# Fused column pairs in five input groups of a one-core encoder layer, turns by way of DRAM, and an account of engine time for the side work

## The chip, the cores and the metric

The kernel runs on one core of one Trainium2 chip. The metric is the device time of one execution in microseconds; the time before is a median of 1603.3 us over three runs (1602.81 to 1603.57). Engines are named as in the profile: PE (matrix products), PEld (its weight loads), DVE (vector), ACT (scalar), POOL (GpSimd) and SP (the queue that issues most DMAs).

## The reference

One layer on x of 256 rows and 4096 columns, all in float32:

```
xn = rms_norm(x) * norm_g
h  = xn @ w_in                                   # 4096 x 14336
c_val, c_glu, c_gate, q, k, v, a_gate = split(h) # 2048 columns each
conv = swish(layer_norm(depthwise_conv31(c_val * sigmoid(c_glu)) + conv_b)) * silu(c_gate)
q, k = rms_norm per head (16 heads of 128)
attn = mixture over three dilated windows of softmax(q k^T / sqrt(128) + bias) v
y    = x + concat(conv, attn * silu(a_gate)) @ w_out   # 4096 x 4096
```

With 256 positions the three patterns and the relative bias become one table by distance, `bias_rows`, added to the scores of each head.

## The kernel before, in words

**Products.** Both large products are cut into groups of 1024 output columns (two halves e of 512): 14 input groups (`GROUPS`: four `conv`, then `agv` and `qk` in turn four times, two `gate`) and four `out` groups. The contraction runs over 32 tiles of 128 (k), two to a pair j; one DMA on SP brings the 1 MB of weights of a pair (`load_pair`, three buffers `raw`). Each float32 operand is split into a rounded high part and a low rest (ACT casts, DVE subtracts: `split_w`, L204 and L205), and a product is three matmuls, high x high, low x high, high x low, in PSUM. An ordinary k-step is 2 row halves x 2 column halves x 3 = 12 matmuls of 128 x 512 (`products`, L662 to L665); a plain pair is 24. The input groups multiply x * norm_g and bring in 1/rms only where PSUM is emptied (`evacuate`). Split tiles have eight slots (`ws`), so three k-steps of weights are split ahead.

**Fused pairs.** In each out group the pairs in `FUSED` (six of 16) are multiplied as 2 x 2 blocks with seven block products instead of eight, 21 matmuls instead of 24. That needs sums of blocks of the left side (`mix_fuse`, tiles `mx`) and of the weights (`split_fused`, steps one to four, with helper tiles `t13` and `t24`), four more PSUM banks (`more`, on the `side` banks in the first out group) and `add_more`, which puts the block sums together. `OUT_ORDERS` says in which order an out group takes its pairs.

**Side work.** The depthwise convolution (`conv_gen`, 31 steps on DVE for each of 16 channel tiles), the norm over channels (`ln_gen`), the norms of q and k (`qk_norm`), the 16 heads (`head_gen`, products `psc` and `po` on `side` banks), the gates (`gate_post`, `ag_post`) and the splits of the mixed result (`mix_split_gen`) are Python generators in four lanes. `pump` is called once in each k-step of the input groups; it adds a fixed quota of DVE and ACT time (`STEP`, `GATE_STEP`) and lets the generators issue until the cost that they report has used it up. The lane `fg` steps its first three generators, in order; the convolution comes last and takes what is left. All engines work strictly in the order in which these instructions are issued; there is no other scheduler.

**Turns.** A tile of rows by columns is turned to columns by rows with a DVE transpose inside blocks of 32 x 32 and then 16 ACT copies that move the blocks (`turn`, L307 and L315; for the probabilities L499 and L505). This is done for four conv tiles, four gates, four attention gates, q and k of four head groups, and the probabilities of 16 heads.

Of the kernel before, what the change touches and what calls it, by code (L numbers as in the profile page):

```python
# [17 lines left out]
P = 128  # L18
# [15 lines left out]
STEP, GATE_STEP = (950, 1400), (1300, 1600)  # L34
AHEAD = 3
RAW = 3
XN_LOAD = {1 + (5 * c + 1) // 2: c for c in range(8)}
# [13 lines left out]
FUSED = (0, 1, 2, 3, 4, 5)  # L51
OUT_ORDERS = [(8, 9, 10, 0, 6, 1, 11, 2, 7, 3, 12, 4, 13, 5, 14, 15)]
OUT_ORDERS += 3 * [(8, 9, 0, 10, 1, 11, 2, 6, 3, 7, 4, 12, 5, 13, 14, 15)]
# [5 lines left out]
def _relative():  # L59
# [4 lines left out]
    for m in range(NDEL):  # L64
        d = m - (S - 1)
# [12 lines left out]
        c = int(n <= 64) + int(n % 4 == 0 and n <= 256) + int(n % 16 == 0 and n <= 1024)  # L78
        pattern[m] = math.log(c) if c else NEG
# [3 lines left out]
class Lane:  # L83


    def __init__(self, width):
        self.gens = deque()
        self.width = width

# [3 lines left out]
    def step(self, left):  # L93

        spent = 0
        for gen in list(self.gens)[: self.width]:
            if min(left) <= 0:
# [7 lines left out]
            for i in range(2):  # L105
                left[i] -= cost[i]
# [5 lines left out]
def layer_kernel(  # L112
# [17 lines left out]
    def t4(name):  # L130
        return sb.tile([P, 4, 256], F32, tag="c4", bufs=15, name=name)
# [13 lines left out]
    def rsqrt(src, shape, mul, eps, name):  # L145
# [6 lines left out]
        cost = 60 + n  # L152
# [24 lines left out]

    raw_tiles = {}

    def load_pair(j, cuts=(0, 2048), between=None):  # L180

        g, jj = divmod(j, n_pairs)
        if g >= NG:
            return
        if groups[g][0] == "out":
            jj = (OUT_ORDERS[g - n_in][jj] + n_pairs // 2) % n_pairs
# [7 lines left out]
    w_split = {}  # L194

    def ws(name):
        return sb.tile([P, 1024], F32R, tag="ws", bufs=W_SLOTS, name=name)

    def split_w(n):
        j, kk = divmod(n, 2)  # L200
        src = raw_tiles[j][:, kk]
        wh, wl = ws(f"wh{n}"), ws(f"wl{n}")
        if n:
            nc.scalar.copy(wh, src)  # L204
            nc.vector.tensor_sub(wl, src, wh.bitcast(F32))  # L205
        else:
            a, b = slice(0, 512), slice(512, 1024)
            nc.vector.tensor_copy(wh[:, a], src[:, a])
            split_x(0)
            nc.scalar.copy(wh[:, b], src[:, b])  # L210
            for c in (a, b):
                nc.vector.tensor_sub(wl[:, c], src[:, c], wh[:, c].bitcast(F32))
        w_split[n] = (wh, wl)
        if kk == 1:
            del raw_tiles[j]
            load_pair(j + RAW)

    xh, xl = {}, {}
# [30 lines left out]
    def split_x(k):  # L249
# [6 lines left out]
        xh[k], xl[k] = h, l  # L256

    state = {}

    def finish_rstd():  # L260
# [5 lines left out]
        state["rstd"] = [keep[:, s : s + 1] for s in range(2)]  # L266

# [24 lines left out]
    def backwards(ap):  # L292

        *lead, (step, n) = ap.ap
        return bass.AP(
            tensor=ap.tensor, offset=ap.offset + (n - 1) * step, ap=[*lead, [-step, n]]
        )

    def turn(tile_, name, flip=False):


# [4 lines left out]
        for s in range(2):  # L306
            nc.vector.transpose(flat[:, 512 * s : 512 * s + 512], src[:, 512 * s : 512 * s + 512])  # L307
            yield 620
        blocks = flat.rearrange("p (s t b x) -> p s t b x", s=2, t=4, b=4)
        dst = src.rearrange("p (t s a x) -> p s t a x", t=4, s=2, a=4)  # L310
        for b in range(4):
            for a in range(4):
                v = blocks[32 * a : 32 * a + 32, :, :, b, :]
                to = 3 - a if flip else a
                nc.scalar.copy(  # L315
                    dst[32 * b : 32 * b + 32, :, :, to, :], backwards(v) if flip else v
                )
            yield 0, 1240
# [7 lines left out]
    def conv_gen(cb):  # L326
# [4 lines left out]
        for tp in range(0, 4, 2):  # L331
            for t in (tp, tp + 1):
# [5 lines left out]
                yield 335  # L338
            for k in range(TAPS):
# [4 lines left out]
                for t in (tp, tp + 1):  # L344
# [5 lines left out]
                    yield 335  # L350
# [4 lines left out]
    def channel_mean(srcs, name):  # L355

        tot = sb.tile([P, S], F32, tag="rs_big", bufs=6, name=name + "tot")
        for i, make in enumerate(srcs):
            v = make()
            if i:  # L360
                part = sb.tile([P, S], F32, tag="rs_big", bufs=6, name=f"{name}p{i}")
            else:
                part = tot
            nc.vector.reduce_sum(part, v.rearrange("p t s -> p s t"), axis=AX.X)
            yield 1135
            if i:
                nc.vector.tensor_add(tot, tot, part)
                yield 335
# [9 lines left out]
    def ln_gen():  # L378
        pm = yield from channel_mean([lambda cb=cb: cT[cb] for cb in range(4)], "mu")
# [3 lines left out]
        for cb in range(4):  # L383
            nc.vector.tensor_sub(cT[cb], cT[cb], bcast4(mu))
            yield 1135

        def square(cb):
            sq = t4(f"sq{cb}")
            nc.scalar.activation(sq, cT[cb], AF.Square)
            return sq  # L390

        pv = yield from channel_mean([lambda cb=cb: square(cb) for cb in range(4)], "va")
        r = yield from rsqrt(pv[:, :S], [P, S], 1.0, LN_EPS, "rc")
        for cb in range(4):
            nc.vector.tensor_mul(cT[cb], cT[cb], bcast4(r))
            yield 1135
        for cb in range(4):
            for t in range(4):
# [5 lines left out]
                if t % 2 == 1:  # L404
                    yield 900
# [4 lines left out]
    def gate_post(cb, g):  # L410
        yield
        yield from turn(g, f"turn_g{cb}")
        while cb not in conv_done:
            yield
        for t in range(4):
            nc.vector.tensor_mul(cT[cb][:, t, :], cT[cb][:, t, :], g[:, t, :])
            mix_ready[NH + 4 * cb + t] = cT[cb][:, t, :]
            yield 335

    def ag_post(hg, ag):  # L420
        yield
        yield from turn(ag, f"turn_ag{hg}")
# [5 lines left out]
    def qk_norm(hg):  # L428
        st = sb.tile([P, 16], F32, tag="rs_small", bufs=6, name=f"ssqk{hg}")
        both = (qt[hg], kt[hg])  # L430
        for i, src in enumerate(both):
            sq = t4(f"sq{hg}_{i}")
            nc.scalar.activation(sq, src, AF.Square)
            yield 0, 1000
            yield
            for s in range(2):
                o = 8 * i + 4 * s
                v = sq.rearrange("p a b -> p (a b)")[:, 512 * s : 512 * s + 512]
                nc.vector.reduce_sum(
                    st[:, o : o + 4], v.rearrange("p (h d) -> p h d", h=4), axis=AX.X  # L440
                )
                yield 600
        r = yield from rsqrt(st, [P, 16], 1.0 / DH, NORM_EPS, f"rqk{hg}")
        for i, src in enumerate(both):
            for s in range(2):
                v = src.rearrange("p a b -> p (a b)")[:, 512 * s : 512 * s + 512]
                v = v.rearrange("p (h d) -> p h d", h=4)
                a = r[:, 8 * i + 4 * s : 8 * i + 4 * s + 4]
                rb = bass.AP(tensor=a.tensor, offset=a.offset, ap=[a.ap[0], [1, 4], [0, DH]])
                nc.vector.tensor_mul(v, v, rb)  # L450
                yield 600
        yield from turn(qt[hg], f"turn_q{hg}", flip=True)
        yield from turn(kt[hg], f"turn_k{hg}")
        yield
        nc.vector.tensor_scalar_mul(kt[hg], kt[hg], gqk)
        yield 650
        qk_ready[hg] = True

    def head_gen(hg, hh):
        h = 4 * hg + hh  # L460
        hs = slice(DH * hh, DH * hh + DH)
        while hg not in qk_ready:
# [6 lines left out]
                offset=bias_dram.offset + h * NDEL,  # L469
# [4 lines left out]
        for it in range(2):  # L474
            nc.tensor.matmul(  # L475
                psc[:, it, :], qt[hg][:, hh, P * it : P * it + P], kt[hg][:, hh, :],
# [5 lines left out]
        window = bass.AP(tensor=T.tensor, offset=T.offset + P, ap=[T.ap[0], [-P, 2], [1, 256]])  # L482
# [4 lines left out]
        yield 1200  # L487
# [5 lines left out]
        yield 0, 700  # L493
        nc.vector.reciprocal(z, z)
        for it in range(2):
            nc.vector.tensor_scalar_mul(pi[:, it, :], pi[:, it, :], z[:, it : it + 1])
        yield 600
        tmp = t2(f"turn_p{h}")
        nc.vector.transpose(tmp, pr)  # L499
        yield 620  # L500
# [507 lines left out]
```

## Time and profile before

| | |
|---|---|
| median of three runs | 1603.3 us |
| the profiled execution, its time / its span | 1603.12 / 1601.3 us |
| PE, PEld busy | 1590.5, 1312.8 us |
| DVE, ACT, POOL busy | 1195.0, 968.2, 0.2 us |
| DMA | 323.53 MB, mean 202 GB/s |
| granted PE clock, mean | 0.998 |

A row of a group of instructions gives line, engine, operation, output<-inputs, shapes and count; then busy us and the mean ns of one; then idle us just before them and what ended most of it. Rows of windows give a stretch in us and for each engine its busy time and number of instructions. A row of DMA issues gives the size of one and the median us from issue to landing. Matmuls are pipelined: the duration of one overlaps the next, and the pace is read from the starts.

### The profile page before, as it was taken

To read this page: it belongs to the slowest core of one execution; us is meant where nothing else is said; L and a number is where in the kernel's file an instruction comes from. 1 tells how busy PE (TensorE), PEld (TensorE's weight loads), DVE (VectorE), ACT (ScalarE), POOL (GpSimd) and SP (SyncE) were. 2 spreads that over 40 slices of the span, in tenths; PEclk is the share of its full clock that TensorE was granted. 3 is DMA by queue.
4 is the path that set the end of the run, shared out by engine and by line. 5 is a ranking of instruction groups with operands and counts; after the bars stand their busy time and mean duration, and the time that the engine had idled before them with its cause. 6 is when DMAs were issued, how large, how long until landed. Compare 5 with 4: busy or idle time off the path is not lost.

```text
span 1601.3 us, 18984 instructions
## 1 busy us (share of the span) xinstructions
PE 1590.5 (99%) x6986; PEld 1312.8 (82%) x6986; DVE 1195.0 (75%) x1630; ACT 968.2 (60%) x1480; POOL 0.2 (0%) x4
## 2 busy tenths in 40 slices
PE   9999999999999999999999999999999999999999
PEld 7888888888888888888888888888878877888887
DVE  6668888888888887678755556555467889888886
ACT  6763534445453467755779557754789865545453
POOL 0000000000000000000000000000000000000000
PEclk9999999999999999999999999999999999999999
DMA  9755555555555555555555555455545556665653
GB/s 377 289 184 198 196 186 201 192 184 207 188 190 204 184 195 191 186 186 191 179 195 189 192 203 190 173 187 207 194 163 190 184 210 232 232 229 215 248 198 143
DMA packets 52892, 323.53 MB, mean 202 GB/s; under 512 B 5792, under 2 KB 8480, under 8 KB 16192
## 3 DMA queue, kind: packets, MB, share of 16 engines
q1 hardware_dynamic: 52512, 322.05, 56.4%
q8 instruction: 54, 0.88, 0.2%
q10 hardware_dynamic: 288, 0.28, 0.1%
q14 instruction: 38, 0.31, 0.1%
HBM read 318.08 MB, written 4.23 MB: 201 GB/s over the span
## 4 chain that ended last, share of the span: by engine, by line
PE 96%; ACT 1%; DVE 1%; issue 0%; DMA 0%; DVEq 0%; ACTq 0%
PE acc L662 25%; PE acc L663 25%; PE acc L665 25%; PE c L784 5%; PE c L782 5%; PE c L783 5%; PE m L784 1%; PE m L782 1%; PE m L783 1%; PE po L514 1%; PE psc L475 1%; ACT gate L315 0%; ACT pr L505 0%; DMA first_x<-in_x_cols_dram 0%; DVE t24l L736 0%
## 5 line engine op out<-in xcount | busy, mean ns | idle before, releaser
L205 DVE TENSOR_TENSOR wl<-raw,wh 128x1024 fp32r<-128x1024 f32 x447 | 546.9, 1224 | 336.9 <-ACT wh L204 335.9
L204 ACT CAST wh<-raw 128x1024 fp32r<-128x1024 f32 x447 | 469.6, 1052 | 434.9 <-PE acc L663 241.5
L662 PE MATMUL acc<-wh,xh 128*128 128x512 f32 x1792 | 703.8, 393 | 1.3 <-ACT xh L252 1.3
L663 PE MATMUL acc<-wh,xl 128*128 128x512 f32 x1792 | 698.4, 390 | 0.0
L665 PE MATMUL acc<-wl,xh 128*128 128x512 f32 x1792 | 483.7, 389 | 0.0
L662 PEld LDWEIGHTS acc<-wh,xh 128*128 128x128 f32 x1792 | 337.0, 188 | 72.3 <-ACT xh L252 1.6
L663 PEld LDWEIGHTS acc<-wh,xl 128*128 128x128 f32 x1792 | 336.8, 188 | 70.1 <-DVE xl L253 0.2
L665 PEld LDWEIGHTS acc<-wl,xh 128*128 128x128 f32 x1792 | 336.3, 188 | 70.3
L346 DVE SCALAR_TENSOR_TENSOR cT<-conv,wT,cT 128x241 f32<-128x241 f32 (+14 forms) x480 | 201.6, 471 | 0.0
L782 PE MATMUL c<-oh,mh 128*128 128x512 f32 x320 | 125.3, 391 | 0.5 <-ACT oh L716 0.5
L784 PE MATMUL c<-ol,mh 128*128 128x512 f32 x320 | 125.1, 391 | 0.5 <-DVE ol L717 0.5
L783 PE MATMUL c<-oh,ml 128*128 128x512 f32 x320 | 125.0, 391 | 0.0
L716 ACT CAST oh<-raw 128x1024 fp32r<-128x1024 f32 x80 | 83.2, 1051 | 50.8 <-PE c L783 34.4
L717 DVE TENSOR_TENSOR ol<-raw,oh 128x1024 fp32r<-128x1024 f32 x80 | 96.1, 1222 | 21.8 <-ACT oh L716 15.2
L505 ACT COPY pr<-turn_p 32x128 f32<-32x128 f32 x256 | 75.9, 297 | 9.2 <-DVE turn_p L499 5.7
L782 PEld LDWEIGHTS c<-oh,mh 128*128 128x128 f32 x320 | 60.5, 189 | 13.5 <-ACT oh L716 1.0
L784 PEld LDWEIGHTS c<-ol,mh 128*128 128x128 f32 x320 | 60.3, 189 | 13.5 <-DVE ol L717 1.0
L783 PEld LDWEIGHTS c<-oh,ml 128*128 128x128 f32 x320 | 60.5, 189 | 12.8
L732 ACT CAST t24h<-t 128x1024 fp32r<-128x1024 f32 x24 | 25.2, 1051 | 40.3 <-PE c L783 24.1
L736 DVE TENSOR_TENSOR t24l<-t,t24h 128x1024 fp32r<-128x1024 f32 x24 | 29.4, 1226 | 17.3 <-ACT t24h L732 17.3
L732 ACT CAST t13h<-t 128x1024 fp32r<-128x1024 f32 x24 | 25.3, 1053 | 18.2 <-DVE t L748 14.2
L732 ACT CAST bh<-raw 128x1024 fp32r<-128x1024 f32 x24 | 25.3, 1053 | 16.3 <-PE m L783 16.3
(195 smaller groups left out, 1030.8 us busy)
## 6 DMA issues: line engine op xcount, KB each, us to landing
raw<-in_w_dram SPq DMA_DIRECT2D x286, 1024.0 KB, 4.8
x<-in_x_dram SPq DMA_DIRECT2D x8, 512.0 KB, 7.4
xr<-in_x_dram SPq DMA_DIRECT2D x8, 512.0 KB, 6.0
out_dram<-xr SPq DMA_DIRECT2D x15, 256.0 KB, 2.9
xT<-in_x_cols_dram SPq DMA_DIRECT2D x7, 512.0 KB, 6.9
T<-bias_dram SPq DMA_DIRECT2D x16, 192.0 KB, 5.0
raw<-in_w_dram SPq DMA_DIRECT2D x3, 512.0 KB, 6.2
raw<-in_w_dram SPq DMA_DIRECT2D x2, 256.0 KB, 4.4
```

Of the source, the lines that this page charges most:

```text
L204: nc.scalar.copy(wh, src)
L205: nc.vector.tensor_sub(wl, src, wh.bitcast(F32))
L346: nc.vector.scalar_tensor_tensor(c[:, t, lo:hi], a[:, t, lo + sh : hi + sh], wT[:, ch, k : k + 1], c[:, t, lo:hi], op0=ALU.mult, op1=ALU.add,)
L505: nc.scalar.copy(dst[32 * b : 32 * b + 32, :, :, 3 - a, :], backwards(blocks[32 * a : 32 * a + 32, :, :, b, :]),)
L662: nc.tensor.matmul(a, hs, wp, start=k == 0, stop=False)
L663: nc.tensor.matmul(a, ls, wp, start=False, stop=False)
L665: nc.tensor.matmul(a, hs, wp, start=False, stop=k == KT - 1)
L716: nc.scalar.copy(h, src)
L717: nc.vector.tensor_sub(l, src, h.bitcast(F32))
L782: nc.tensor.matmul(acc, a[0], b[0], start=start, stop=False)
L783: nc.tensor.matmul(acc, a[1], b[0], start=False, stop=False)
L784: nc.tensor.matmul(acc, a[0], b[1], start=False, stop=stop)
```

## The change

1. The input groups 2 to 6 (`FUSED_IN`) take the pairs 2, 4, 6, 8 as fused pairs. The first out group fuses two pairs (0 and 1) instead of six, the other three six as before; the order of the first out group is new. One class `Stream` now splits all weights, of plain groups too.
2. Block sums across rows need normalized x. So in group 1 x is loaded again (eight DMAs of 512 KB), scaled by norm_g and by 1/rms in a row (which goes out to DRAM and comes back to all partitions), split again (`split_xn`), and the sums are made (`block_sums`). From group 2 on nothing is scaled when PSUM is emptied. A fused input group uses all eight PSUM banks; `evacuate_sum` adds the last banks to what `add_more` left.
3. The heads start only once the fused input groups are done (`state["side"]`), since these use the `side` banks.
4. Turns of q, k, both gates and the probabilities go through DRAM: DVE transposes the blocks, then POOL issues one write and four reads (`through_dram`); the generator gives way five times (`LANDING`) before the result is used. The conv tiles keep the ACT copies.
5. The quotas are replaced by an account: each matmul credits 0.93 of 227 ns to DVE and to ACT (`credit`), every instruction, the weight splits too, is taken off (`spend`), and at most 700 ns are carried over. The reported costs are raised.
6. The norms of q and k and the scaling of q and of the probabilities move from DVE to ACT; the sums over channels are additions of whole tiles instead of reductions; `t13` and `t24` are written in place into `raw`; helper tiles `c4` are 18 instead of 15, the DMA scratch is smaller; 11 warm-up products instead of 7; the load of x for the output sums stands at slot 7 instead of 9.

```diff
-STEP, GATE_STEP = (950, 1400), (1300, 1600)
+PRODUCT = 227
+FILL, SAVED = (0.93, 0.93), (700, 700)
+LANDING = 5
+C4 = 18
...
-FUSED = (0, 1, 2, 3, 4, 5)
-OUT_ORDERS = [(8, 9, 10, 0, 6, 1, 11, 2, 7, 3, 12, 4, 13, 5, 14, 15)]
+FUSED_IN = range(2, 7)
+FUSED = [(2, 4, 6, 8) if g in FUSED_IN else () for g in range(N_IN)] + [range(2)] + 3 * [range(6)]
+ORDERS = N_IN * [range(16)]
+ORDERS += [(8, 9, 10, 11, 6, 7, 2, 3, 0, 12, 1, 13, 14, 4, 5, 15)]
...
+    def credit(ns):
+        for i in range(2):
+            left[i] += FILL[i] * ns
...
+    def split_xn(k):
+        src = xT[k]
+        nc.vector.scalar_tensor_tensor(
+            src, src, g_cols[:, k : k + 1], state["rstd_row"], op0=ALU.mult, op1=ALU.mult
+        )
+        yield 480
+        h, l = new_split(k, "n")
+        nc.scalar.copy(h, src)
+        yield 0, 400
+        nc.vector.tensor_sub(l, src, h.bitcast(F32))
+        xh[k], xl[k] = h, l
+        yield 415
+        if k % 2 and k // 2 in FUSED[FUSED_IN[0]]:
+            yield from block_sums(k // 2, src_of=xT, parts=(xh, xl), out=xsum, name="xs")
...
+    def through_dram(src, dst, n, name):
+        d = tc.dram_tile([P, 4 * n], F32, name=name + "d")
+        nc.gpsimd.dma_start(d, src)
+        for b in range(4):
+            nc.gpsimd.dma_start(
+                dst[32 * b : 32 * b + 32, :].rearrange("p (a n) -> p a n", a=4),
+                bass.AP(
+                    tensor=d.tensor,
+                    offset=d.offset + b * n,
+                    ap=[[4 * n, 32], [P * n, 4], [1, n]],
+                ),
+            )
+        for _ in range(LANDING):
+            yield
...
-        while hg not in qk_ready:
+        while hg not in qk_ready or not state["side"]:
             yield
...
-        blocks = tmp.rearrange("p (i j b x) -> p j i b x", i=2, j=2, b=4)
-        dst = pr.rearrange("p (j i a x) -> p j i a x", j=2, i=2, a=4)
-        for b in range(4):
-            for a in range(4):
-                nc.scalar.copy(
-                    dst[32 * b : 32 * b + 32, :, :, 3 - a, :],
-                    backwards(blocks[32 * a : 32 * a + 32, :, :, b, :]),
-                )
-            yield 0, 800
+        yield 700
+        yield from through_dram(tmp, pr, 128, f"turn_p{h}")
...
+    def pump(more=0):
+        credit(more)
+        gate_lane.step(left, spend)
+        fg.step(left, spend)
         for _ in range(2):
-            mix_lane.step(left)
+            mix_lane.step(left, spend)
         for _ in range(8):
-            if not conv_lane.step(left):
+            if not conv_lane.step(left, spend):
                 break
+        for i in range(2):
+            left[i] = min(left[i], SAVED[i])
...
             def one():
-                t13 = kept["t13"] = t4(f"t13_{u}").rearrange("p a b -> p (a b)").rearrange(
-                nc.vector.tensor_sub(t13, r[:, 1:4:2, :], r[:, 0:2, :])
+                both("b", r[:, 0:3:2, :], ("b11", "b21"))
+                nc.vector.tensor_add(r[:, 0:2, :], r[:, 0:2, :], r[:, 1:4:2, :])
+                spend(1225)
...
+            if g == FUSED_IN[0] - 1:
+                if k % 4 == 0:
+                    load_xT(k, 4, nc.sync)
+                if k >= 2:
+                    split_gens.append(split_xn(k - 2))
+                split_more()
             pump()
```

More of the change, by code (lines that the diff above doesn't have):

```diff
@@ L104, in step @@
             cost = cost if isinstance(cost, tuple) else (cost, 0)
-            for i in range(2):
-                left[i] -= cost[i]
+            spend(*cost)
             spent += sum(cost)
@@ L192, in load_pair @@
                 between()
[L194 to L218, printed above, removed]
+    xh, xl, xsum = {}, {}, {}
     def new_split(k, nm):
@@ L452, in qk_norm @@
[L452 to L456, printed above, removed]
+            v = src.rearrange("p a b -> p (a b)")
+            for n in range(8):
+                w_ = v[:, DH * n : DH * n + DH]
+                nc.scalar.activation(
+                    w_, w_, AF.Copy, scale=r[:, 8 * i + n : 8 * i + n + 1]
+                )
+                if n % 4 == 3:
+                    yield 0, 1600
@@ L698, in free, with step @@
                 self.held[tag] -= 1
[L700 to L702 removed]
+        def step(self):
+            if not self.todo or sum(self.held.values()) + self.todo[0][0] > W_SLOTS + self.more:
                 return False
@@ L781, in triple, with bank @@
+            def four():
+                both("t24", blocks()[:, 0:2, :], ("t2", "t4"))
+            return [(2, one), (1, two), (2, three), (2, four)]
+        def bank(self, g, name, tag):
+            return ps.tile([P, 512], F32, tag=tag, bufs=4, name=f"{name}_{g}")
         def triple(self, acc, a, b, start, stop):
@@ L948, in layer_kernel @@
     progress["in"] = KT + 2
-    out.run()
+    mix_lane.engines = ()
+    for g in range(n_in, NG):
+        stream.group(g)
 def _layout(i):
```

632 lines of the change are left out of this document (359 added, 273 removed).

## The prediction

> **What bounds the kernel now.** I read the page first: how busy the engines are, the chain that ended last, the costliest groups.
>
> ```profile
> span 1601.3 us, 18984 instructions
> PE 1590.5 (99%) x6986; PEld 1312.8 (82%) x6986; DVE 1195.0 (75%) x1630; ACT 968.2 (60%) x1480; POOL 0.2 (0%) x4
> PE 96%; ACT 1%; DVE 1%; issue 0%; DMA 0%; DVEq 0%; ACTq 0%
> L205 DVE TENSOR_TENSOR wl<-raw,wh 128x1024 fp32r<-128x1024 f32 x447 | 546.9, 1224 | 336.9 <-ACT wh L204 335.9
> L204 ACT CAST wh<-raw 128x1024 fp32r<-128x1024 f32 x447 | 469.6, 1052 | 434.9 <-PE acc L663 241.5
> ```
>
> 96% of the chain is matrix work; DVE and ACT are 75% and 60% busy and mostly wait for PE to free a slot. Next the chain in order of time, for the pace:
>
> ```profile
> 16.12 0.91 PE acc L665 x4
> 18.84 0.91 PE acc L665 x4
> 609.98 1.73 PE psc L475 x8
> ```
>
> A k-step of 12 matmuls takes 18.84 - 16.12 = 2.72 us, so one matmul costs 0.2267 us. 5376 of them in the 14 input groups and 1464 in the output groups are 1550.4 us of the span. Then windows, for where that pace is lost:
>
> ```profile
> 200.00:300.00 100.00, 100.00 (x443) 82.80 (x442) 85.17 (x139) 46.64 (x56) 0.00 (x0) 1.00 0.54 190
> 1100.00:1200.00 100.00, 99.48 (x438) 81.70 (x438) 57.61 (x77) 71.95 (x132) 0.00 (x0) 1.00 0.53 185
> 1274.00:1300.00 26.00, 23.84 (x94) 18.13 (x93) 23.73 (x34) 15.98 (x26) 0.00 (x0) 0.93 0.45 161
> 1300.00:1340.00 40.00, 38.56 (x167) 30.71 (x167) 34.91 (x41) 29.70 (x45) 0.00 (x0) 1.00 0.60 214
> 1340.00:1423.00 83.00, 83.00 (x368) 68.73 (x367) 74.39 (x83) 42.74 (x45) 0.00 (x0) 1.00 0.67 239
> ```
>
> The columns are busy time and instructions of PE, weight load, DVE, ACT and POOL, then clock and DMA. An input group runs at 443 matmuls per 100 us with DVE 85% busy, an output group with six fused pairs at 368 per 83 us with DVE at 74.4 of 83: neither loses anything. Only the first output group does.
>
> ```profile
> 5.73 0.80 PE L662 MATMUL acc<-wh,xh 128*128 128x512 f32 x1 [1.33 <-ACT xh L252]
> 1257.76 0.39 PE L782 MATMUL c<-oh,mh 128*128 128x512 f32 x1
> 1596.98 0.39 PE L784 MATMUL c<-ol,mh 128*128 128x512 f32 x1
> ```
>
> From 1257.76 to 1597.21 (the last start and one pace) are 339.4 us for 1464 x 0.2267 = 331.9 us: 7.6 us lost, nearly all between 1274 and 1340, where DVE is 23.7 of 26 us busy with six fused splits begun at the fourth pair, while the last mixes are still being made.
>
> **Part by part.** *Matmuls.* A fused pair needs 21 instead of 24. Five input groups with four each: -60. The first output group goes from six fused pairs to two: +12. Net -48 x 0.2267 = **-10.9 us**, all on PE's path. The heads keep their 64 matmuls.
>
> *First output group.* Its two fused pairs stand at slots 8 and 10. Prices of DVE's pieces:
>
> ```profile
> L736 DVE TENSOR_TENSOR t24l<-t,t24h 128x1024 fp32r<-128x1024 f32 x24 | 29.4, 1226 | 17.3 <-ACT t24h L732 17.3
> L759 DVE TENSOR_TENSOR t<-raw,t 128x512 f32<-128x512 f32 x24 | 16.4, 684 | 0.0
> L560 DVE TENSOR_TENSOR mix_sums<-mix_sums,agv 128x128 f32<-128x128 f32 x6 | 1.8, 292 | 0.2
> L548 DVE TENSOR_TENSOR ml<-cT,mh 128x256 fp32r<-128x256 f32 x16 | 6.6, 418 | 0.7
> L499 DVE STREAM_TRANSPOSE turn_p<-pr 128x512 f32<-128x512 f32 x16 | 11.2, 703 | 0.0
> ```
>
> A fused split is 4 x 1.226 + 3 x 0.684 = 6.96 us of DVE, a plain pair 2.45. So 2 x 6.96 + 14 x 2.45 = 48.2 us of weights. Beside them stand 16 x 0.418 for the last gates and mixes, 4 transposes at 0.70, the sums of four pairs at 1.85 (4 x 0.292 + 0.684) and 12 additions at 0.684, 25 us: 73 in 378 x 0.2267 = 85.7 us, a smaller share than the 74.4 in 83 that cost nothing. Of the 7.6 us I take 4 back (ends 0 and 7.6): **-4**.
>
> *DVE in the fused input groups.* 4 x 6.96 + 12 x 2.45 = 57.2 us of weights and 5.5 to 8.2 for putting the sums together, in 372 x 0.2267 = 84.3 us. The new account gives every matmul 0.93 x 227 = 211 ns of each engine and takes every instruction off it, so side work can fill DVE to 93% only; in the fused stretch (9.41 us of splits per 10.2 us) it gets nearly nothing. The second output group ran such an alternation at no loss, covered by the tiles split ahead: 0. Without that cover the last fused pair of a stretch, 6.96 us of splits against 21 x 0.2267 = 4.76 us of products, is 2.2 us late, 11 us in five groups.
>
> *Group 1.* Each x tile is loaded again, scaled, and split; four pairs get sums.
>
> ```profile
> L253 DVE SCALAR_TENSOR_TENSOR xl<-xT,first_x,xh 128x256 fp32r<-128x256 f32 x31 | 14.8, 479 | 0.7 <-ACT xh L252 0.7
> xT<-in_x_cols_dram SPq DMA_DIRECT2D x7, 512.0 KB, 6.9
> bias_dram<-tb SPq DMA_DIRECT2D x1, 32.0 KB, 4.3
> raw<-in_w_dram SPq DMA_DIRECT2D x286, 1024.0 KB, 4.8
> ```
>
> DVE: 32 x (0.479 + 0.418) = 28.7, sums 4 x (4 x 0.292 + 0.684) = 7.4, weights 39.2, turn and evacuation 3, leftovers 3: 81 of 87.0 us. A load is issued two k-steps (5.4 us) before its first use and lands in 6.9 behind a weight load, so DVE may wait 1.5 us eight times: 93 us against 87, less the two k-steps of weights split ahead. I take **+2** (0 to 8). The row of 1/rms goes through DRAM on SP; its read waits about 4.3 us for the write, with weight loads queued behind. Those have 10.9 - 4.8 = 6.1 us in hand: 0. The load of x for the output sums, two slots earlier on SP, is hidden by the same 6.1 us: 0.
>
> *Turns through DRAM.* These remove 512 small ACT copies and cost POOL, until now idle, a write and four reads for each of 16 tiles and 16 heads: 160 issues, which queue in order. Each first read waits there for its own write to land, and the next turn's write stands behind. The consumer comes five calls of the planner later.
>
> ```profile
> L505 ACT COPY pr<-turn_p 32x128 f32<-32x128 f32 x256 | 75.9, 297 | 9.2 <-DVE turn_p L499 5.7
> T<-bias_dram SPq DMA_DIRECT2D x16, 192.0 KB, 5.0
> out_dram<-xr SPq DMA_DIRECT2D x15, 256.0 KB, 2.9
> ```
>
> ACT's saving is worth 0, since ACT waits for PE. For a head the nearest rows are 2.9 us (write of 256 KB) and 5.0 (read): 7.9 us, between 2 x 2.9 = 5.8 and 2 x 6.9 = 13.8. Counted from its transpose, the product with the values comes six calls later, 6 x 2.72 = 16.3 us; alone it always lands in time. Three heads go at once, but the account keeps their transposes apart, the second one call later: it lands after 2 x 7.9 = 15.8 us and is due at 19.0. So no stall at 7.9, and one where the trip exceeds 9.5. A head behind a 512 KB turn of the next group will be late sometimes: **+3** (0 to 46, which is R2 at 13.8). PE itself waits there, so this counts in full. q and k have a spare call more.
>
> By the Trainium skill, "DMA: Bandwidth & Descriptors", section "Anatomy of one DMA — SWDGE (gpsimd) path", a DMA from this queue costs about 2.0 us plus its bytes at 436 GB/s; a head's trip would be 5.2 us by estimate, and the 3 us would go. No run here shows that queue yet.
>
> *Waits for the heads.* Heads start only with group 7, when the fused groups have left the side banks: 16 in seven groups of 32 calls, about 13 calls for three. 0.
>
> *The convolution* gets what is left of the account.
>
> ```profile
> L346 DVE SCALAR_TENSOR_TENSOR cT<-conv,wT,cT 128x241 f32<-128x241 f32 (+14 forms) x480 | 201.6, 471 | 0.0
> ```
>
> A plain group credits 384 x 0.211 = 81.1 us, less 39.2 for weights: 41.9; a fused one leaves 14 to 16. Less turns, evacuations and heads this gives the convolution 3 + 67 us up to group 6, then 28, 27, 39, 27, 39: 230 us by the end of group 11 for 480 x 0.47 + 16 x 0.41 = 232. The normalization over channels (some 22 us, 14 passes over 1024 columns at 1.22 and small ones) fits group 12, with some 25 us of margin in group 13. 0.
>
> *Start.* Four more warm-up matmuls:
>
> ```profile
> 1.04 3.36 PE L900 MATMUL spin<-ones 128*128 128x128 f32 x14 [1.04 <-DVE ones L143]
> ```
>
> 22 records end near 6.3 us instead of 4.4, 0.6 after the first product could start, and may spare part of its slow first 3 us: 0 (-1 to +0.6).
>
> **Sum** against the profiled execution: 1601.3 - 10.9 - 4 + 2 + 3 = 1591.4 us of span. That execution took 1603.12, so 1.8 lies around the span: 1593.2. It is 0.2 under the median of 1603.3. Forecast **1593 us**, 10 less.
>
> **Rivals.** *R1, all gain.* Nothing lands late and the whole 7.6 us comes back: 1603.1 - 10.9 - 7.6 = 1585. For: the settled windows lose nothing. Against: new work in group 1.
>
> *R2, slower: late heads.* If a turn holds POOL and lands after 12 us, the second head of each three is 2 x 12 - 19.0 = 5 us late; 5.3 such threes give 27 us on top of the sum without its 3: 1593 - 3 + 27 = 1617. From 9.5 us a trip costs; at 10.7 the gain is gone: (2 x 10.7 - 19.0) x 5.3 = 13. For: xT's 6.9 us. Against: 2.9 and 5.0. A stall also costs clock:
>
> ```profile
> 1285.00:1290.00 5.00, 3.79 (x15) 2.36 (x13) 4.54 (x9) 2.76 (x5) 0.00 (x0) 1.00 0.26 82
> 1290.00:1295.00 5.00, 4.25 (x12) 3.06 (x13) 4.80 (x5) 3.07 (x5) 0.00 (x0) 0.72 0.52 200
> ```
>
> Thinned to 15 and 12 matmuls, PE ran at 0.72. "TensorE: Matmul & The Clock Gate" of the Trainium skill, Part 1, has the clock halve after an idle window of some 3.4 us; the trace shows the drop after less than that.
>
> *R3, POOL held up by DVE.* If each of a turn's five issues waits for one DVE instruction (1.2 us), a trip is 7.9 + 6 = 13.9, the second head 8.8 us late, 47 us in all: 1637.
>
> ```profile
> L455 DVE TENSOR_SCALAR qk<-qk,gqk 128x1024 f32<-128x1024 f32 x4 | 3.0, 748 | 0.0
> ```
>
> For R3: DVE will be up to 93% full where the heads run. Against: this quick kind of instruction (748 ns for 1024 elements, where two inputs take 1224) and the probabilities' scaling move to ACT. The Trainium skill has such a trap in "SBUF — State Buffer", section "SBUF: two separate sides": a DMA from GpSimd starves while DVE runs an instruction on both of its ports, such as a copy of fp32 within SBUF. No run here shows it; by that rule only the quick kind would count.
>
> *R4, group 1 eats the gain.* Its upper end, and nothing back in the output group: 1603.1 - 10.9 + 8 + 3 = 1603, no change.
>
> *R5, late normalization.* Its 25 us margin used up and 15 more: PE waits at 1258: 1608.
>
> **How the numbers follow.** Forecast 0.60 (own range 1587 to 1599), R1 0.10, R2 0.10, R3 0.03, R4 0.12, R5 0.05. The 8-in-10 range leaves out half of R1, R2 and R3 but for a little, and half of R5: 1585 to 1607. About 0.2% (3.2 us) can be told from no change. Faster (under 1600.1): 0.60 + 0.10 + a quarter of R4 = 0.73; same: three quarters of R4 and a little of R2 = 0.11; slower 0.16.
>
> **What would show it.** 6792 full matmuls at an unchanged 2.72 us per 12; the fused input groups near 84.3 us; in the first output group fewer than 4 us lost; PE's waits on the probabilities' tile under 5 us in sum, on the first layer-norm product none. Wrong it is if PE's waits name a DMA from POOL, or DVE in group 1 waits for xT long enough that PE's count falls below 443 per 100 us.

## The result: slower by 1.7%, and the profile after

The changed kernel took 1629.9 us (median; 1628.9 to 1632.4) beside 1603.1 for the kernel before: a ratio of 1.0169, 95% interval 1.0152 to 1.0187. The forecast was 1593. The profiled execution took 1628.9 us, of which 1627.1 are span. One execution of the first experiment below took 3246 us, twice the others, and is left out there. First the page of the changed kernel, its rows for the span, the engines and the chain:

```profile
span 1627.1 us, 19224 instructions
PE 1590.6 (98%) x6946; PEld 1305.8 (80%) x6946; DVE 1273.7 (78%) x1752; ACT 868.8 (53%) x1254; POOL 88.0 (5%) x164
PE 17%; DVE 5%; ACT 2%; issue 1%; DMA 0%; POOL 0%; DVEq 0%; ACTq 0%
```

The count of matmul records is the announced one (6986 - 48 + 8 warm-ups = 6946), and still the span is 25.8 us longer. Beside 17% for PE the chain now has DVE and ACT; its shares add up to 25% only, so it speaks for a quarter of the span, and the rest has to be found by windows (columns as before):

```profile
180.00:265.00 85.00, 82.65 (x360) 66.81 (x359) 73.27 (x95) 48.75 (x66) 0.00 (x0) 1.00 0.58 213
265.00:350.00 85.00, 85.00 (x376) 70.19 (x375) 74.03 (x94) 47.51 (x61) 0.00 (x0) 1.00 0.54 200
1180.00:1190.00 10.00, 2.20 (x5) 1.82 (x6) 2.22 (x3) 9.64 (x17) 0.00 (x0) 0.59 0.01 1
```

The second fused input group runs at full pace, 376 matmuls in 85 us; the first has 360. In 1180 to 1190 there are five matmuls, and it is ACT that is full. And PE's waits by the instruction waited for (sum, times, longest):

```profile
PE acc L760 <- ACT wh L815: 13.3, 3, 9.3
PE m L883 <- DVE t24l L846: 5.6, 14, 0.5
PE acc L760 <- ACT agv L699: 5.6, 2, 2.9
PE po L603 <- DMA pr<-turn_p6d: 1.4, 1, 1.4
```

To put every microsecond in a place, take PE's starts one after another and subtract 0.2267 us for each matmul (the few of 256 and 128 columns, heads and warm-ups, are counted at the same price). What is left over:

| stretch (us) | before | after | what PE waits for there, after |
|---|---|---|---|
| start | 2.9 | 0.6 | |
| 100 to 120 | - | 3.6 | the x tiles loaded again (group 1) |
| 180 to 620 | - | 6.4 | `t24l`, `t24h` of the fused input pairs |
| 780 to 1000 | 0.5 | 11.2 | the emptying of two `agv` groups, one landing |
| 1160 to 1240 | 1.6 | 19.1 | the gate group: mostly weight casts, late on ACT |
| first out group | 7.6 | 2.6 | |
| later out groups | - | 4.2 | `t24l` |
| all | 13.7 | 48.8 | |

(The rest of each sum is spread in small pieces.) 48.8 - 13.7 = 35.1 lost, 10.9 saved by the 48 matmuls, and 1.8 for the eight more warm-ups at that price come to 26.0, beside the 25.8 that the spans differ by.

### The profile page after: what moved, and what is told of

Read it like the earlier page. It is cut to its first block, busy times and chain, and to the rows that moved or that the text cites. A ratio compares the mean times of both kernels' runs of the same rounds, so it can differ in the third digit from the quotient of the medians.

```text
span 1627.1 us, 19224 instructions
## 1 busy us (share of the span) xinstructions
PE 1590.6 (98%) x6946; PEld 1305.8 (80%) x6946; DVE 1273.7 (78%) x1752; ACT 868.8 (53%) x1254; POOL 88.0 (5%) x164
## 5 line engine op out<-in xcount | busy, mean ns | idle before, releaser
L760 PE MATMUL acc<-wh,nh 128*128 128x512 f32 x896 | 358.1, 400 | 18.6 <-ACT wh L815 12.0
L761 PE MATMUL acc<-wh,nl 128*128 128x512 f32 x896 | 352.1, 393 | 0.0
L763 PE MATMUL acc<-wl,nh 128*128 128x512 f32 x896 | 243.6, 391 | 1.4 <-DVE wl L816 1.4
L760 PEld LDWEIGHTS acc<-wh,nh 128*128 128x128 f32 x896 | 170.0, 190 | 56.3 <-ACT wh L815 12.9
L761 PEld LDWEIGHTS acc<-wh,nl 128*128 128x128 f32 x896 | 170.1, 190 | 35.4
L883 PE MATMUL c<-wl,nh 128*128 128x512 f32 x480 | 186.9, 389 | 0.0
L882 PE MATMUL c<-wh,nl 128*128 128x512 f32 x480 | 186.8, 389 | 0.0
L881 PE MATMUL c<-wh,nh 128*128 128x512 f32 x480 | 186.7, 389 | 0.0
L881 PEld LDWEIGHTS c<-wh,nh 128*128 128x128 f32 x480 | 90.1, 188 | 18.6
L760 PE MATMUL acc<-wh,xh 128*128 128x512 f32 x256 | 100.3, 392 | 1.6 <-ACT wh L815 1.3
L761 PE MATMUL acc<-wh,xl 128*128 128x512 f32 x256 | 99.7, 390 | 0.0
```

Of the source, the lines that this page charges most:

```text
L760: nc.tensor.matmul(a, hs, wp, start=k == 0, stop=False)
L761: nc.tensor.matmul(a, ls, wp, start=False, stop=False)
L763: nc.tensor.matmul(a, hs, wp, start=False, stop=k == KT - 1)
L881: nc.tensor.matmul(acc, a[0], b[0], start=start, stop=False)
L882: nc.tensor.matmul(acc, a[1], b[0], start=False, stop=False)
L883: nc.tensor.matmul(acc, a[0], b[1], start=False, stop=stop)
```

## Four places in the trace

*The largest wait.* ACT in the changed kernel, in order of time (start, duration):

```profile
1175.15 1.28 ACT L582 ACT_TABLE_LOAD   x1
1177.55 1.28 ACT L485 ACT_TABLE_LOAD   x1
1178.84 7.97 ACT L485 ACTIVATE cT<-cT,vec_cols 128x256 f32<-128x256 f32 x16
1186.72 2.92 ACT L815 CAST wh<-raw 128x1024 fp32r<-128x1024 f32 x3
```

and PE:

```profile
1187.80 0.79 PE L760 MATMUL acc<-wh,nh 128*128 128x512 f32 x1 [9.26 <-ACT wh L815]
```

All 16 swishes of the normalized convolution come in one piece, two table loads ahead of them, and the next weight cast stands behind. `ln_gen` reports them as `yield 0, 1200`, but the convolution's lane is `Lane(1, (0,))`: it looks at DVE's account alone, and `pump` steps it up to eight times. Eight steps that cost DVE nothing are let through in one call, however deep ACT is in debt.

A second wait for a weight cast, 2.8 us at 1215.48, has another cause. DVE waits for the landing of a gate's turn:

```profile
1212.46 0.42 DVE L502 TENSOR_TENSOR cT<-cT,gate 128x256 f32<-128x256 f32 x1 [6.70 <-DMA gate<-turn_g1d]
```

ACT stands still for 9.8 us until DVE has made `z` for the next head, and the cast comes behind that. So a late landing also reaches PE by way of DVE and ACT, where PE's waits don't name it.

*The fused pairs.* DVE, one fused pair of the first fused input group:

```profile
206.47 1.23 DVE L846 TENSOR_TENSOR t13l<-raw,t13h 128x1024 fp32r<-128x1024 f32 x1 [0.57 <-ACT t13h L845]
207.73 0.69 DVE L868 TENSOR_TENSOR raw<-raw 128x512 f32<-128x512 f32 x1
208.45 0.69 DVE L869 TENSOR_TENSOR raw<-raw 128x512 f32<-128x512 f32 x1
210.32 1.23 DVE L846 TENSOR_TENSOR t24l<-raw,t24h 128x1024 fp32r<-128x1024 f32 x1 [1.18 <-ACT t24h L845]
```

The sums for `t24` (L868, L869) overwrite `raw`, so they can't start until `t13l` has read it; then ACT casts, with DVE idle 1.18 us, and only then comes `t24l`. In the old kernel the sums had helper tiles of their own.

*The end of an `agv` group.* Its emptying needs the table of the swish, which a small activation (L1069) loads ahead of time. ACT in the changed kernel:

```profile
789.02 1.28 ACT L1069 ACT_TABLE_LOAD   x1
790.54 1.28 ACT L582 ACT_TABLE_LOAD   x1
797.21 1.28 ACT L699 ACT_TABLE_LOAD   x1
798.51 1.09 ACT L699 ACTIVATE agv<-acc 128x512 f32<-128x512 f32 x2
```

Between the two, heads come with their exponentials (L582) and throw the table out; it is loaded again while PE waits for the banks, 2.7 and 2.9 us in two such groups, 5.6 in all.

*The turns.* POOL while three heads are turned, in the changed kernel:

```profile
803.32 0.56 POOL L356 DMA_DIRECT2D turn_p4d<-turn_p  x1 [28.93 <-DVE z L587]
806.28 2.18 POOL L358 DMA_DIRECT2D pr<-turn_p4d  x4 [2.40 <-ACT wh L815]
808.45 0.56 POOL L356 DMA_DIRECT2D turn_p5d<-turn_p  x1
814.11 2.19 POOL L358 DMA_DIRECT2D pr<-turn_p5d  x4 [5.10 <-ACT pr L589]
816.84 0.56 POOL L356 DMA_DIRECT2D turn_p6d<-turn_p  x1 [0.54 <-DVE turn_p L594]
826.98 2.24 POOL L358 DMA_DIRECT2D pr<-turn_p6d  x4 [9.57 <-ACT wh L815]
```

with the DMAs' own times from issue to landing (last column):

```profile
turn_p4d<-turn_p POOLq DMA_DIRECT2D x1, 256.0 KB, 2.3
turn_p5d<-turn_p POOLq DMA_DIRECT2D x1, 256.0 KB, 4.8
turn_p6d<-turn_p POOLq DMA_DIRECT2D x1, 256.0 KB, 9.6
```

and for the write and the four reads of p5 together:

```profile
DMA to landing us min/median/max: 3.7/4.3/6.8
```

The engines named as releasers on POOL had long been done; it waits for its own write. p4's write lands in 2.3 us, p5's, right behind p4's reads, in 4.8, and p6's in 9.6. The place behind other reads doesn't settle it: p3's write, with nothing of POOL's ahead of it, took 5.0. A trip ends with the last of its reads, not with the median one. p5's last read is issued at 815.75 and lands after 6.8 us, 19.2 us after p4's write. p6 is written at 816.84; its reads are issued between 826.98 and 829.22, and the last lands at 834.2, 17.3 us after the write.

## The experiments

The kernel before took 1602.9 to 1603.3 us beside each of these, so the medians can be set side by side. All compute the whole layer.

**E1 to E4: one part of the changed kernel each.** E1 puts the swishes on DVE's account as well, so that only a few pass in one call:

```diff
-                    yield 0, 1200
+                    yield 1200, 1200
```

> The 16 swishes of the channel norm report their cost to DVE's account as well as ACT's, so the convolution's lane, which looks at DVE's account alone, issues two to four of them per call instead of all 16. Theory A (side work is issued to ACT in clumps ahead of the casts of the weights): the gap of PE at 1177 us and the slow clock behind it, 13.0 us in sum, go, and with them some of the 6 us lost after 1200 us: 1611 to 1618 us. Theory B (the turns through DRAM land too late) and theory C (the fused input groups overfill DVE): the gap stays or reappears elsewhere, 1626 to 1631 us.

1626.9, 1627.9 and 1631.2 us: ratio 1.0166 (1.0146 to 1.0186). No gain that can be told. The 9.3 us wait is gone, but the next late thing takes its place: PE waits 6.1 us for the landing of p12.

E2 takes the fused input pairs out:

```diff
-FUSED = [(2, 4, 6, 8) if g in FUSED_IN else () for g in range(N_IN)] + [range(2)] + 3 * [range(6)]
+FUSED = [() for g in range(N_IN)] + [range(2)] + 3 * [range(6)]
```

> Groups 2 to 6 run as plain groups on normalized x, no block sums are made for them; all the rest is as changed. 60 matmuls more, 13.6 us. Theory C: the losses were brought by the fused groups and go with them, 1605 to 1615 us. Theories A and B: only the 6 us lost in groups 2 to 6 go and the other losses stay in number, though they come earlier: about 1637 us.

1672.7 us, 1.0439 (1.0424 to 1.0455): 43 slower than the changed kernel, for 13.6 us of matmuls. PE's waits:

```profile
PE po L603 <- DMA pr<-turn_p12d: 15.0, 1, 15.0
PE po L603 <- DMA pr<-turn_p11d: 6.6, 1, 6.6
```

Late landings stand first, once the heads fall at other moments. So turns in a row do reach PE, and how often is a matter of when the heads run.

E3 gives a landing nine calls of the planner instead of five:

```diff
-LANDING = 5
+LANDING = 9
```

> Each turn through DRAM gives way nine calls of the planner instead of five before its result is used. Theory B: PE's waits for the probabilities and the waits of the gates' multiplication on their DMA go, 6 to 10 us, 1620 to 1624 us. Theory A: the gaps at 797, 985 and 1177 us stay, since no DMA is in them; at most 3 us, 1626 to 1631 us, or slower if the last heads come too late for the first output group.

1618.3 us, 1.0094 (1.0079 to 1.0109): 11.6 back, though in the changed kernel PE waited for landings for 1.7 us in all. What went are the 5.6 us on `agv` and most of the 13.3 us on weight casts (1.6 left); what came are 12.3 us for p15, behind the gates, and 4.5 for the emptying of a gate group, behind the swishes. The `agv` group of above, ACT in E3's trace:

```profile
786.60 1.28 ACT L1069 ACT_TABLE_LOAD   x1
790.28 1.09 ACT L699 ACTIVATE agv<-acc 128x512 f32<-128x512 f32 x2 [0.98 <-PE acc L763]
```

No exponential stands between the two any more, the table is loaded once, and it is ACT that waits for PE. So `LANDING` also moves the heads against the ends of the groups.

E4 replaces every turn through DRAM by 16 ACT copies, as before the change:

```diff
-        d = tc.dram_tile([P, 4 * n], F32, name=name + "d")
-        nc.gpsimd.dma_start(d, src)
...
+            for a in range(4):
+                nc.scalar.copy(
+                    dst[32 * b : 32 * b + 32, a * n : a * n + n],
+                    src[32 * a : 32 * a + 32, b * n : b * n + n],
+                )
+            yield 0, 1610 if n == 256 else 1190
```

> The turns go by 16 copies on ACT again (same layout as the turns through DRAM), reported to the account; POOL issues nothing. 512 copies are some 155 us more of ACT, which is 869 of 1627 us busy. Theory B: without landings the 8 us of waits on DMA go, 1620 us. Theory A: the copies are more work in front of the casts, so the gaps stay or grow, 1630 to 1650 us.

1639.7 us, 1.0229 (1.0214 to 1.0245): 9.9 slower. The way through DRAM isn't the fault as such; with copies PE waits 14.1 us for them at `po`.

**E5 to E8: three edits together, and what is left.** E5 is the changed kernel with LANDING 9, E1's spread, and another order of the first out group:

```diff
-ORDERS += [(8, 9, 10, 11, 6, 7, 2, 3, 0, 12, 1, 13, 14, 4, 5, 15)]
+ORDERS += [(8, 9, 10, 11, 2, 3, 4, 5, 6, 7, 0, 12, 1, 13, 14, 15)]
```

> Nine calls for a landing, the swishes spread, and the last heads' pairs (6 and 7) at slots 8 and 9 of the first output group instead of 4 and 5, so that the last head has 22 us more. If late landings and clumps on ACT are separate causes, both savings add to those of the longer landing alone (1618 us): the wait of 12.3 us on the last head and the 4.7 us on the gates' evacuation go, 1601 to 1604 us. If the losses only move (a late thing is late wherever it stands), 1610 us or more.

1614.8 us, 1.0071 (1.0056 to 1.0086). E6 is E5 with the heads' exponentials, and the scaling of the probabilities behind them, held back in the last four k-steps of the groups whose emptying needs another table:

```diff
+        while state["hold"]:
+            yield
...
+            state["hold"] = k >= KT - 4 and groups[g][0] in EVAC_TABLE
```

> As the three together, and in the last four k-steps of a gate group no exponential and no scaling of probabilities is issued, so that the evacuation finds ACT free and its table loaded. If clumps at group ends still cost: 2 to 5 us less than the three together. If the longer landing already moved the heads off the group ends: no difference.

1613.0 us, 1.0059 (1.0041 to 1.0076), between 1605.8 and 1617.4: not to be told from E5.

E7 is E5 with `t13` and `t24` in helper tiles, and `t24` summed before `t13` is split:

```diff
-                nc.vector.tensor_add(r[:, 0:2, :], r[:, 0:2, :], r[:, 1:4:2, :])
+                nc.vector.tensor_add(kept["t13"], r[:, 0:2, :], r[:, 1:4:2, :])
...
-                both("t13", r[:, 0:2, :], ("t1", "t3"))
-                nc.vector.tensor_add(r[:, 0, :], r[:, 0, :], r[:, 3, :])
-                nc.vector.tensor_add(r[:, 1, :], r[:, 0, :], r[:, 2, :])
+                nc.vector.tensor_add(t24[:, 0, :], t13[:, 0, :], r[:, 3, :])
+                nc.vector.tensor_add(t24[:, 1, :], t24[:, 0, :], r[:, 2, :])
+                both("t13", t13, ("t1", "t3"))
```

> As the three together, and the two sums of a fused weight split go to helper tiles, made one step ahead of their cast as in the kernel before, instead of in place into raw right before it. Theory: the 3.9 us lost in groups 2 to 3 and the 4 us in the last three output groups come from ACT waiting for DVE's sum in place (77 + 75 us of ACT waits); then 4 to 7 us less than the three together. Rival: DVE is too full there; then no difference.

1598.0 us, 0.9970 (0.9957 to 0.9983): 16.8 less than E5, far more than expected. The group of instructions in the changed kernel and in E7, and then the window of the first fused input group in E7:

```profile
L846 DVE TENSOR_TENSOR t24l<-raw,t24h 128x1024 fp32r<-128x1024 f32 x40 | 49.0, 1226 | 46.4 <-ACT t24h L845 46.4
L847 DVE TENSOR_TENSOR t24l<-t,t24h 128x1024 fp32r<-128x1024 f32 x40 | 49.0, 1226 | 6.0 <-ACT t24h L846 4.5
```

```profile
180.00:265.00 85.00, 85.00 (x376) 70.43 (x375) 75.70 (x98) 49.90 (x66) 0.00 (x0) 1.00 0.59 217
```

In the changed kernel DVE idles 46.4 us ahead of the same 40 `t24l`; here 6.0, and all five fused input groups run at 376 matmuls per 85 us. By the starts E5 lost 35.2 us and E7 17.2. Of these 18, 6.2 are in the fused input groups, 7.3 at 1380 to 1420 in the second out group, where E5 also waited 4.5 us for the cast of a sum (`msp`), which stands behind a `t24l` in DVE's order, and 3.6 behind that.

E8 is E5 with the three DMAs of the row of 1/rms on POOL's queue instead of SP's:

```diff
-        nc.sync.dma_start(
+        nc.gpsimd.dma_start(
```

> As the three together, and the row of 1/rms goes through DRAM on POOL's queue instead of SP's, so SP does not stand still at 93 us. If the 3 to 4 us lost at 110 us come from weight and x loads issued in one burst behind that wait: 2 to 4 us less than the three together. If x's reload is late by itself (6.9 us against 5.4): no difference.

1616.3 us, 1.0082 (1.0067 to 1.0097): nothing gained. The loss at 100 to 120 us falls from 2.1 to 1.2 us and doesn't matter.

**E9: the best version.** E7's one large wait is for head 15. POOL, and PE's wait, in E7:

```profile
1260.42 0.56 POOL L356 DMA_DIRECT2D turn_g3d<-turn_g  x1
1268.90 2.19 POOL L358 DMA_DIRECT2D gate<-turn_g3d  x4 [7.92 <-issue]
1271.08 0.56 POOL L356 DMA_DIRECT2D turn_p15d<-turn_p  x1
1278.44 2.18 POOL L358 DMA_DIRECT2D pr<-turn_p15d  x4 [6.80 <-ACT mh L633]
```

```profile
PE po L603 <- DMA pr<-turn_p15d: 8.0, 1, 8.0
```

Two gates of 512 KB stand ahead of it in the queue, and they aren't needed before the head is. E9 lets them go last:

```diff
+        while cb >= 2 and fg.gens:
+            yield
         yield from turn_far(g, f"turn_g{cb}")
```

> As the version with the longer landing, spread swishes, the last heads later and helper tiles (1598 us), and the turns of the last two gates wait until all heads are done, so that the last head's turn no longer stands behind their two 512 KB turns on POOL. If POOL's order makes the last head late (its write was issued at 1271 us, behind both), the 8.0 us wait at 1279 us and the loss behind it go: 1588 to 1590 us. If the landing itself is slow there: 1595 us or more.

1594.8 us (1593.0 to 1596.5), 0.9949 (0.9937 to 0.9962): 3.1 less than E7 and 8.2 less than the kernel before. Its span and chain, and the largest of PE's waits:

```profile
span 1591.3 us, 19219 instructions
PE 94%; DVE 2%; DMA 2%; ACT 1%; issue 1%; SPq 0%; DVEq 0%; ACTq 0%
```

```profile
PE c L891 <- ACT mh L635: 2.5, 1, 2.5
```

PE is the chain again (94%), no landing stands among its waits, and 12.9 us are lost instead of 48.8. The 8.0 us wait is gone as expected, but the gain over E7 is 3.1 us and not 8 to 10: with the gates last, PE now waits 2.5 us for a mixed tile that needs one of them.

**E10 to E12: each part put back into E9.** What a part is worth shows only where nothing else is late. E10 puts the clump of swishes back:

```diff
-                    yield 1200, 1200
+                    yield 0, 1200
```

> As the gates-last version, with the 16 swishes issued in one call again, as in the changed kernel. It prices the clump where nothing else is late: theory A, 5 to 13 us more than the gates-last version; if the clump hurt only because other things were late too, under 2 us more.

1603.4 us, 1.0005 (0.9996 to 1.0015): the clump costs 8.6. The largest wait is now for the emptying of a gate group, which stands behind the 16 swishes on ACT:

```profile
PE acc L762 <- ACT gate L701: 4.5, 1, 4.5
```

E11 puts the five calls back:

```diff
-LANDING = 9
+LANDING = 5
```

> As the gates-last version, with five calls for a landing again. It prices the short landing where nothing else is late: theory B, 8 to 18 us more than the gates-last version, with PE's waits on the probabilities' DMA and group ends that fall together with the heads' ACT work; if the short landing only hurt behind clumps, under 3 us.

1613.5 us, 1.0066 (1.0052 to 1.0079): 18.6 slower. PE's waits:

```profile
PE po L605 <- DMA pr<-turn_p12d: 6.1, 1, 6.1
PE acc L762 <- ACT agv L701: 5.3, 2, 2.7
PE acc L762 <- ACT wh L817: 4.6, 2, 3.4
```

With p13's 2.1 and the small ones, 9.2 us of it are landings; the other half is ACT: the exponentials lie between the table's load and its use again, as in the changed kernel, and among the swishes (E9 waits 1.3 us for weight casts and not at all for `agv`). E12 takes the fused input pairs out of E9, with E2's edit:

> As the gates-last version, with groups 2 to 6 plain, on normalized x and with no block sums. If the fused input groups now run at PE's pace, this is 60 x 0.2267 = 13.6 us slower than the gates-last version. If they still cost something of their own, less than that.

1609.8 us, 1.0045 (1.0031 to 1.0059): 15.0 slower, for 60 matmuls x 0.2267 = 13.6. So in E9 the fused groups cost nothing of their own.

**E13 to E15.** E13 is the changed kernel with E7's helper tiles alone:

> The changed kernel with helper tiles for the sums of the fused weight splits and nothing else altered. If the causes add, it gains what the in-place sums cost between the two versions with the longer landing (16.8 us): 1613 us. If that cost depended on the longer landing and the new order, only the 10 us that PE's gaps show in the fused groups: 1619 us.

1617.4 us, 1.0088 (1.0072 to 1.0103): 12.5 back, between the two. What stays are the waits for weight casts (14.2 us) and for `agv` (5.3). E14 is E9 with E4's copies:

> The gates-last version with ACT copies instead of turns through DRAM (no landing, no POOL). If the turns through DRAM are worth what they take off ACT once nothing waits for them: 3 to 10 us slower than the gates-last version (1595 us). If ACT has room for the 155 us, as the sum of the prediction said: no difference, 1593 to 1597 us.

1613.7 us, 1.0066 (1.0052 to 1.0080): 18.8 slower than E9. The same window of the gate group in E9 and in E14:

```profile
1180.00:1190.00 10.00, 10.00 (x46) 8.29 (x45) 7.03 (x10) 4.88 (x5) 0.00 (x0) 1.00 0.78 205
1180.00:1190.00 10.00, 5.96 (x25) 4.31 (x24) 2.45 (x2) 9.77 (x22) 0.00 (x0) 1.00 0.29 106
```

ACT is 65% busy over the span, but 9.77 of 10 us where the copies of a gate, the swishes and the casts of weights meet, and PE has 25 matmuls instead of E9's 46. E15 is E9 with the fused pairs 0 and 1 one slot earlier each in the first out group, and 7 and 12 one later:

```diff
-ORDERS += [(8, 9, 10, 11, 2, 3, 4, 5, 6, 7, 0, 12, 1, 13, 14, 15)]
+ORDERS += [(8, 9, 10, 11, 2, 3, 4, 5, 6, 0, 7, 1, 12, 13, 14, 15)]
```

> The gates-last version with the pairs of the last gates (12 and 13) one slot later and pair 7 between the two fused ones in the first output group. If the 3.5 us lost at 1304 us come from the last gates' mixes being late behind POOL: 2 to 3 us less, 1592 us. If from DVE being full there: no difference.

1600.5 us, 0.9984 (0.9975 to 0.9992): 5.6 slower. PE's wait:

```profile
PE c L891 <- ACT mh L635: 6.8, 1, 6.8
```

Neither expectation holds: the wait is 6.8 us instead of 2.5, though pair 12, whose mixed tile is late, stands a slot later than in E9. Both fused pairs are now done ahead of it, and DVE makes eight of their sums, from 1311.24, before the gate's multiplication that the tile needs: that starts at 1316.16 instead of 1305.72 in E9.

## Why the prediction was wrong, by its own steps

Three steps failed that made the kernel slower. *DVE in the fused input groups* went in at 0 and left out that the sums are made in place: 12.5 us (E13). *The turns* went in at +3 with a trip of 7.9 us; the heads' trips took 7.6 to 17.3, and five calls instead of nine cost 11.6 us (E3). *The convolution* went in at 0 by DVE's account alone, and the swishes behind it hold up ACT: 8.6 us where little else is late (E10). All steps in their order:

*The matmuls* (-10.9): right. The count is as announced, and E12 has 15.0 for the 60 in the input groups.

*The first out group* (-4): right, 7.6 us lost before and 2.6 after.

*Group 1* (+2): 3.6 us lost, of the kind named (DVE waits for the x tiles), and PE's count falls to 426 per 100 us from 95 to 195, one of the two signs of being wrong that the prediction names; the other, a DMA of POOL's among PE's waits, came too. The row of 1/rms on SP at 0: right, by E8.

*The start* (0): right. The settled pace is reached 0.7 us earlier than before: the eight more warm-ups take 1.0 us, and of 2.9 us of waiting and slow first products 1.4 stay (the 0.6 of the table has the warm-ups at 0.2267 us each, more than they took).

*DVE in the fused input groups* (0): wrong. The step priced busy time and took its cover from the old second out group, whose sums were in helper tiles. The same change had the sums made in place, listed but priced nowhere; 6.4 us were lost here and 4.2 in the later out groups, none of which lost anything before. The price of the edit is 12.5 us alone (E13), 16.8 beside E5's edits. That DVE has the time was right: with helper tiles the fused groups lose nothing, with DVE 75.7 of 85 us busy.

*The turns* (+3, up to 46): the mechanism was named and the direct cost was small (1.7 us at `po`, where under 5 was forecast). But the trip was mis-sized. Against the 7.9 us of the sum the heads' trips took 7.6 to 17.3 us, p4's with POOL free 9.6. The second of two heads landed 15.8 us (p1) to 19.2 us (p5) after the first one's write, where 15.8 was forecast and 19.0 was due; that PE waited only 0.3 us for p5 is luck. Left out were the engines other than PE that wait for a landing (DVE 6.7 us for a gate, and PE 2.8 behind it), and what a landing is worth that isn't late but displaced: five calls against nine are 11.6 us in the changed kernel (E3) and 18.6 in E9 (E11), there half landings and half ACT's work in other places. Heads behind gates, which the 3 us were for, cost 8.0 us for p15 in E7 and 6.1 for p12 in E1 and E11. Rival R2, given one chance in ten, had a trip of 12 us, nearer to these, but the 27 us that it put on the second heads didn't come.

*Waits for the heads* (0): no run tests the later start by itself. The first head's product stands at 649 us, 609.8 before, and the last one's product with the values at 1269, 1240 before.

*ACT's saving at 0, "since ACT waits for PE"*: wrong in the other direction; without the saving the changed kernel takes 9.9 us more (E4) and E9 18.8 (E14). The mean of 60% was read where the stage decides; the gate group is where ACT ends last.

*The convolution* (0, with 25 us of margin): the data were in time, and R5 didn't come. But the step looked at DVE's account alone, as the lane does. The 16 swishes in one piece cost 8.6 us where nothing else is late (E10), and nothing that can be told in the changed kernel (E1), since p12 is next.

R3 shows no sign in POOL's issues: four reads take 2.17 to 2.25 us throughout. A hold-up by DVE that shows only in the landing isn't excluded; it wasn't tried apart. R4 was 3.6 of 8 us.

E9, in which little side work is late, took 1594.8, near the forecast of 1593; but it isn't the kernel that was forecast. From the changed kernel to E9, in the order of the runs: the landing 11.6 (E3), swishes and order 3.5 (E5), helper tiles 16.8 (E7), gates last 3.1 (E9), together 35.0. The parts hide each other: 8.6 us of swishes show as none in E1.

What stays open: why a write of 256 KB lands in 2.3 us in one place and in 9.6 in another. Between 822.5 and 827 us, while p6's write is awaited, POOL's queue moves five packets, 0.02 MB, beside 0.90 MB of weight loads on SP's: the write waits for its last few packets, and what holds those back (the reads ahead, the weight loads) was not separated. Open is also how much of E11's 18.6 us another start of the heads would win with five calls. The order in E5 was not run without the other two edits.

## What to carry to other kernels

Where several things wait behind one in-order queue, price each part with the others mended: one edit alone may show nothing while it is worth 8 us. An account that paces side work has to look at every engine on which the bounding engine's next operand stands, even for pieces that cost the watched engine nothing. And a tile reused in place is a wait: ask which read it has to follow before its bytes are called free.

## What the runs showed of the hardware

A short wait can cost PE more than its length. At the emptying of an `agv` group in the changed kernel, PE waits 2.67 us, and then:

```profile
799.16 0.59 PE L760 MATMUL acc<-wh,nh 128*128 128x512 f32 x1 [2.67 <-ACT agv L699]
799.54 0.63 PE L761 MATMUL acc<-wh,nl 128*128 128x512 f32 x1
802.91 0.39 PE L761 MATMUL acc<-wh,nl 128*128 128x512 f32 x1
```

From 799.54 the starts are 0.43 us apart instead of 0.2267, until 802.91, at a granted clock of 0.50 (800 to 802 us): the nine matmuls from 799.16 on take some 1.7 us more, on top of the wait. After the 9.26 us wait at 1187.80 it is the same pace for about as long. The length of the wait alone doesn't decide. E13 has the same one without it:

```profile
979.74 0.50 PE L760 MATMUL acc<-wh,nh 128*128 128x512 f32 x1 [2.67 <-ACT agv L699]
```

The next starts follow 0.34 and 0.23 us later. And E14 has a wait of 2.35 us twice, at 1188.76 without the slow starts and at 1194.12 with them. "TensorE: Matmul & The Clock Gate" of the Trainium skill, Part 1, has the halving after an idle window of some 3.4 us; here 2.67 us were enough in one place and not in another.

The page "DMA: Bandwidth & Descriptors" of the Trainium skill, section "Anatomy of one DMA — SWDGE (gpsimd) path", gives some 2.6 us for a write of 256 KB on this queue by estimate. p4's took 2.3; the 5.0 us of p3's, also alone, and the 4.8 and 9.6 us behind other turns are not in it.
